# A two-layer hybrid trunk on one core: x loaded first, work ahead of the first matmuls reordered, softplus moved to GpSimd

## The chip, the cores and the metric

The kernel runs on one NeuronCore of a Trainium2 chip. The metric is the device time of one execution in microseconds; lower is better. Engines are called as the profile calls them: PE (TensorE matmul), PEld (its weight loads), DVE (VectorE), ACT (ScalarE), POOL (GpSimd) and SP (SyncE, which here only issues DMAs).

## What is computed

Two layers, 256 positions, width 1024. The part that matters here is the way into a layer and the first things that are made of its projection:

```python
c_act = silu(c)
# per layer
mod = c_act @ ada_w + ada_b;  shift, scale, gate = split(mod, 3)
h = rmsnorm(x, norm_g) * (1 + scale) + shift
z = h @ w_in                       # 13312 columns; all branches read z
q = rope(rmsnorm(b_q, qn_g), pos) * 0.125;  k = rope(rmsnorm(b_k, kn_g), pos)
log_a = -8 * sigmoid(...) * softplus(-lru_lambda)    # RG-LRU branch
...
x = x + gate * (merged @ w_o)
```

Behind z stand three branches: a convolution with a gated recurrence (A), attention over dilated windows (B) and gated linear attention (C). They are multiplied with further weights and merged.

## The kernel before

x is kept transposed: 8 tiles of 128 features by 256 positions. All weights are read once. `stream` cuts them into units in the order of use, which SP loads into six `raw` buffers (512 KB each at most). For each unit ACT makes a rounded copy `whi` (L223) and DVE the rest `wlo` (L224); h is split in the same way into `hhi` and `hlo`, and each product is three matmuls (whi by hhi, wlo by hhi, whi by hlo). `advance` does this split up to three units ahead.

The first 16 units are the columns for q, k, v and the gate of branch B of head pair 0, four pieces of the contraction each (`mm_t`, L789 to 791; `xps` tiles for the gate, L777 to 779). Each piece needs two of the eight tiles of h. The next units are of kind F (`mm_f`, L797 to 799): one unit gives one tile of 128 columns for branch A (`ax`, `ag`).

**adaLN.** The rows of c_act @ ada_w are not made on PE: for each of 16 columns `ada_tile` runs one DVE instruction over a 128 by 1024 weight tile (L325, shown as a custom instruction and a read of its accumulator), then a small product (L327). Columns come in pairs (shift, scale); a pair completes one tile of h: `h_tile` does `tmp` on DVE (L357), `hhi` on ACT (L359), `hlo` on DVE (L360). START spreads the 16 columns over the first 13 units; ten of them land in early buffers named after later tiles (`ada_yhi`, `ada_ylo`, `ada_hraw` and so on).

**rms.** `stats_start` squares x on ACT (L372), adds on DVE (L375, L376) and sums over partitions on PE (L379). `rstd_full` makes the inverse root: `rs_y` on ACT by logarithm and exponential, then a correction with `rs_m` and `rs_q` on DVE (L342, L346 to 348).

**Small constants.** `angles` (L412 to 427) reduces position times frequency and takes sine and cosine; `rope_tables` (L436 to 443) makes eight products of 128 by 192. `softplus` (L390 to 404) is 19 DVE instructions on 128 by 16 with one exponential on ACT. Its results `sp4` and `sp4n` are first used by branch A.

**Evacuation of q and k** (`evac_qk`, L552 to 560). For each half of the positions DVE multiplies the PSUM bank with two tables into `ra` and `rb` (two buffers each) and reduces the squares to `ss`; POOL adds `ra` and `rb` into `ro` (L557, L558), scales `ss` (L559) and takes its power (L560); DVE multiplies `ro` with it (L565). There are four such halves for pair 0 (q twice, then k twice). F units write the PSUM banks that these halves free (pool `pmm`, 4 banks).

**Order.** A scheduler that simulates time puts the instructions of each engine in a row; an engine runs its row in order and waits at its head. `tc.issue_after` only forces an order between two instructions. SP issues loads in the order written, as buffers come free.

## Time and profile before

| | us |
|---|---|
| median of 3 runs | 910.96 (910.28 to 912.53) |
| the profiled execution | 912.47 |
| its span, first to last instruction | 910.7 |
| PE busy in the span | 872.9 (96%) |
| DVE busy | 673.0 (74%) |
| ACT busy | 532.0 (58%) |
| POOL busy | 175.1 (19%) |
| mean granted TensorE clock | 0.996 of full speed |

The span is cut into 40 slices of some 23 us, and the digits below are tenths of busy time in each. PE is full everywhere but in the first slice; DVE is nearly full in the first four.

```profile
## 2 busy tenths in 40 slices
PE   3989999999999999999999999989999999999998
PEld 3978999999988888999889999989999988899998
DVE  6998898669666667666775888986896666656674
```

### The profile page before, as it was taken

The numbers are of one execution on the slowest core, as the hardware profiler recorded it, in microseconds if no ns is written. First come the engines' busy times: TensorE is split into PE (matmuls) and PEld (weight loads), VectorE is DVE, ScalarE is ACT, GpSimd is POOL, SyncE is SP. The second block draws the span as 40 slices with busy tenths as digits, with TensorE's granted clock in tenths as the row PEclk, the third lists the DMA queues.
The fourth block names the chain that finished last, engine by engine and source line by source line (L and its number), as shares of the span: only waits on it lengthen the run. The fifth ranks groups of instructions, "written<-read, shape, count | busy, mean of one in ns | idle before, by whom it ended". The sixth has DMA issues, their size and how long they took to land.

```text
span 910.7 us, 16407 instructions
## 1 busy us (share of the span) xinstructions
PE 872.9 (96%) x6340; PEld 825.3 (91%) x6340; DVE 673.0 (74%) x1115; ACT 532.0 (58%) x897; POOL 175.1 (19%) x160
## 2 busy tenths in 40 slices
PE   3989999999999999999999999989999999999998
PEld 3978999999988888999889999989999988899998
DVE  6998898669666667666775888986896666656674
...
GB/s 328 317 279 139 145 165 207 132 136 201 240 189 191 202 212 205 208 238 206 224 152 160 177 145 145 179 195 109 190 206 232 160 190 163 150 173 185 188 163 47
DMA packets 52111, 170.16 MB, mean 187 GB/s; under 512 B 6240, under 2 KB 8160, under 8 KB 52032
## 3 DMA queue, kind: packets, MB, share of 16 engines
...
q0 software_dynamic: 144, 0.20, 0.2%
...
## 4 chain that ended last, share of the span: by engine, by line
PE 57%; DVE 18%; DMA 10%; issue 7%; ACT 5%; POOL 3%; SPq 0%; DVEq 0%; ACTq 0%
PE mm L797 10%; PE mm L799 10%; PE mm L798 10%; DMA raw<-in_ada_dram 8%; DVE wlo L224 7%; PE mm L791 6%; PE mm L790 6%; PE mm L789 6%; PE xps L172 1%; ACT whi L223 1%; POOL ss L560 1%; PE xps L168 1%; DVE raw L325 1%; DVE rb L554 1%; DVE ra L552 1%
## 5 line engine op out<-in xcount | busy, mean ns | idle before, releaser
L224 DVE TENSOR_TENSOR wlo<-raw,whi 128x1024 fp32r<-128x1024 f32 (+2 forms) x288 | 335.6, 1173 | 86.9 <-ACT whi L223 85.5
L223 ACT CAST whi<-raw 128x1024 fp32r<-128x1024 f32 (+2 forms) x288 | 280.2, 977 | 189.5 <-PE mm L798 123.6
L797 PE MATMUL mm<-hhi,whi 128*128 128x256 f32 x768 | 217.8, 284 | 3.3 <-DVE rb L554 3.2
L799 PE MATMUL mm<-hhi,wlo 128*128 128x256 f32 x768 | 216.6, 282 | 3.1 <-DVE wlo L224 3.1
L798 PE MATMUL mm<-hlo,whi 128*128 128x256 f32 x768 | 216.0, 281 | 0.0
L789 PE MATMUL mm<-whi,hhi 128*128 128x384 f32 (+2 forms) x480 | 170.9, 361 | 7.2 <-ACT hhi L359 6.5
L790 PE MATMUL mm<-wlo,hhi 128*128 128x384 f32 (+2 forms) x480 | 173.0, 362 | 1.4 <-DVE wlo L224 1.2
L791 PE MATMUL mm<-whi,hlo 128*128 128x384 f32 (+2 forms) x480 | 169.1, 358 | 0.5 <-DVE hlo L360 0.5
L797 PEld LDWEIGHTS mm<-hhi,whi 128*128 128x128 f32 x768 | 144.6, 188 | 5.3 <-ACT tmp L847 3.6
L799 PEld LDWEIGHTS mm<-hhi,wlo 128*128 128x128 f32 x768 | 144.5, 188 | 4.3 <-DVE wlo L224 3.7
L798 PEld LDWEIGHTS mm<-hlo,whi 128*128 128x128 f32 x768 | 144.8, 189 | 0.4
L789 PEld LDWEIGHTS mm<-whi,hhi 128*128 128x128 f32 x480 | 93.4, 195 | 15.3 <-ACT hhi L359 7.9
L790 PEld LDWEIGHTS mm<-wlo,hhi 128*128 128x128 f32 x480 | 93.9, 196 | 9.1 <-DVE wlo L224 2.8
L325 DVE CUSTOM_DVE_ANT_0 raw<-raw,crow,vec_sb 128x1024 f32<-128x1024 f32 x38 | 48.7, 1283 | 70.7 <-DMA raw<-in_ada_dram 70.7
L791 PEld LDWEIGHTS mm<-whi,hlo 128*128 128x128 f32 x480 | 92.7, 194 | 7.2 <-DVE hlo L360 0.8
L797 PE MATMUL mm<-yhi,whi 128*128 128x256 f32 x320 | 89.9, 281 | 2.1 <-DVE mg L939 2.1
L798 PE MATMUL mm<-ylo,whi 128*128 128x256 f32 x320 | 89.3, 279 | 0.0
L799 PE MATMUL mm<-yhi,wlo 128*128 128x256 f32 x320 | 89.2, 279 | 0.0
L797 PEld LDWEIGHTS mm<-yhi,whi 128*128 128x128 f32 x320 | 60.4, 189 | 3.1 <-DVE mg L939 2.3
L799 PEld LDWEIGHTS mm<-yhi,wlo 128*128 128x128 f32 x320 | 60.2, 188 | 0.8 <-DVE mrg L905 0.8
L798 PEld LDWEIGHTS mm<-ylo,whi 128*128 128x128 f32 x320 | 60.1, 188 | 0.0
L698 POOL TENSOR_TENSOR at_hl<-att_sb,at_hl 128x384 fp32r<-128x384 f32 x8 | 8.8, 1096 | 207.1 <-ACT at_hl L697 207.1
...
## 6 DMA issues: line engine op xcount, KB each, us to landing
raw<-in_ws_dram SPq DMA_DIRECT2D x192, 512.0 KB, 4.0
...
```

The source lines that it names most:

```text
L168: seen[0] = T.matmul(*a, **k).ins
L172: seen[0] = T.transpose(*a, **k).ins
L223: A.copy(hi, r)
L224: V.tensor_tensor(lo, r, hi.bitcast(F32), ALU.subtract)
L325: V.tensor_tensor_reduce(w, w, crow2, 1.0, b, ALU.mult, ALU.add, a if i == 0 else m)
L552: V.tensor_tensor(ra.rearrange("p (g s) d -> p g s d", g=3), z4, ctab[l][:, i, t].unsqueeze(2).to_broadcast(bc), ALU.mult)
L789: T.matmul(o, ah, wh, start=(k == 0), stop=False)
L790: T.matmul(o, ah, wl, start=False, stop=False)
L791: T.matmul(o, al, wh, start=False, stop=(k == KT - 1))
L797: T.matmul(ps[:, 0:S], hi[:, a:b], xh[:, k], start=(k == 0), stop=False)
L798: T.matmul(ps[:, 0:S], hi[:, a:b], xl[:, k], start=False, stop=False)
L799: T.matmul(ps[:, 0:S], lo[:, a:b], xh[:, k], start=False, stop=(k == nk - 1))
```

## The change

Six things are changed, all in the first tenth of the program (layer 1 keeps its code).

- The three small loads `eye`, `pos` and `inv` go out on the ACT queue, ahead of ACT's table load; on SP x follows c at once. `pos` and `inv` had been loaded by SP behind the fourth adaLN column.
- `angles` keeps the reduction and runs between `diag` and the sums of squares; `sines` has the sine, the cosine and what follows. The eight table products of 192 columns become four of 384.
- Adding 1 to the scale biases (`b1`) moves behind the sums of squares.
- For layer 0 columns 2 to 15 of adaLN, and the `wlo` of units 0 to 3, are ordered behind the first `tmp` of h; the `whi` of units 1 to 3 behind the first `hhi`.
- `softplus` runs on GpSimd but for one reciprocal on DVE and three ACT functions, and is started at unit 4 in place of 16. Multiply-and-add pairs become two instructions, as GpSimd gets single operations. The scaling of `vec_sb` at V_ON goes to GpSimd too.
- `warm_up` gives PE two matmuls on `diag` and three on `rs_m`, whose results nobody reads.

```diff
@@ advance
-                    if it[1] < 4:
-                        st.enter_context(tc.issue_after(cur["ra"]))
-                        st.enter_context(tc.issue_after(cur["rv"]))
+                    if it[1] < 4:
+                        st.enter_context(tc.issue_after(cur["h0a" if it[1] else "ra"]))
                     A.copy(hi, r)
+                with ExitStack() as st:
+                    if it[1] < 4:
+                        st.enter_context(tc.issue_after(cur["h0v"]))
                     V.tensor_tensor(lo, r, hi.bitcast(F32), ALU.subtract)
@@ loads
-    SY.dma_start(out=eye_sb, in_=eye)
+    for t, s in ((eye_sb, eye), (pos_sb, pos), (inv_sb, inv.partition_broadcast(P))):
+        A.dma_start(out=t, in_=s)
@@ ada_tile
+        with ExitStack() as st:
+            if l == 0 and 2 <= c < 16:
+                st.enter_context(tc.issue_after(cur["h0v"]))
+            V.tensor_tensor_reduce(w, w, crow2, 1.0, b, ALU.mult, ALU.add, a if i == 0 else m)
@@ stats_start
-                V.tensor_tensor(sq[i - 1], sq[i - 1], t, ALU.add)
-        V.tensor_tensor(sq[0], sq[0], sq[2], ALU.add)
+                with tc.issue_after(cur["an"]):
+                    V.tensor_tensor(sq[i - 1], sq[i - 1], t, ALU.add)
+        v = V.tensor_tensor(sq[0], sq[0], sq[2], ALU.add)
+        b1 = vec_sb[:, :, V_ADA:V_ADA + 16].rearrange("p l (j i) -> p l j i", i=2)[:, :, :, 0]
+        with tc.issue_after(v.ins):
+            V.tensor_scalar(b1, b1, 1.0, None, ALU.add)
@@ softplus
-        V.scalar_tensor_tensor(e, lam, -1.0, lam, ALU.mult, ALU.max)
+        A.activation(e, lam, AF.Abs)
         A.activation(e, e, AF.Exp, scale=-1.0)
-        V.tensor_scalar(s, e, 2.0, None, ALU.add)
+        G.tensor_scalar(s, e, 2.0, None, ALU.add)
         V.reciprocal(s, s)
-        V.tensor_scalar(p, s2, 1.0 / 17.0, None, ALU.mult)
-        for k in range(7, 0, -1):
-            V.scalar_tensor_tensor(p, p, 1.0 / (2 * k + 1), s2, ALU.add, ALU.mult)
+        G.tensor_scalar(p, s2, 1.0 / 17.0, 1.0 / 15.0, ALU.mult, ALU.add)
+        for k in range(6, -1, -1):
+            G.tensor_tensor(p, p, s2, ALU.mult)
+            G.tensor_scalar(p, p, 1.0 / (2 * k + 1), None, ALU.add)
...
@@ rope_tables
-            for t in range(2):
-                V.tensor_tensor(ct[:, i, t].rearrange("p g (e d) -> p g e d", e=2), g,
-                                cs[:, t].unsqueeze(1).unsqueeze(1).to_broadcast([P, 3, 2, 32]), ALU.mult)
+            V.tensor_tensor(ct[:, i].rearrange("p t g (e d) -> p t (g e) d", e=2),
+                            g.unsqueeze(1).to_broadcast([P, 2, 6, 32]),
+                            cs.unsqueeze(2).to_broadcast([P, 2, 6, 32]), ALU.mult)
...
@@ start of the program
+    with tc.issue_after(cur["diag"]):
+        angles()
+    warm_up(diag[:, 0:2].rearrange("p k n -> p (k n)"), 2)
     sts = stats_start()
-    rstd = rstd_full(sts)
+    rstd = rstd_full(sts, 3)
...
-    sts = layer(0, h, {2: tables, 15: load_small, 16: small})
+    sts = layer(0, h, {2: tables, 4: small, 15: load_small})
```

**DVE at the start**, between the sum over partitions and the first tile of h. `ada_yhi` and `ada_ylo` are adaLN columns 0 to 3 and ISA is the adaLN instruction; before:

```order
L342 TENSOR_SCALAR rs_m<-xps 128x256
L325 ISA ada_ylo,acc<-ada_ylo,crow,vec_sb 128x1024
L325 ISA acc 128x1
L346 TENSOR_TENSOR rs_q<-rs_y 128x256
L325 ISA ada_ylo,mod<-ada_ylo,crow,vec_sb 128x1024
L325 ISA mod 128x1
L327 TENSOR_TENSOR mod<-acc,vec_sb 128x1
L347 TENSOR_TENSOR rs_q<-rs_q,rs_m 128x256
L348 SCALAR_TENSOR_TENSOR rs_y<-rs_q,rs_y 128x256
L224 TENSOR_TENSOR wlo<-raw,whi 128x800
L357 SCALAR_TENSOR_TENSOR tmp<-x_sb,mod,rs_y 128x256 x2
```

The same place on DVE after the change:

```order
L346 TENSOR_SCALAR rs_m<-xps 128x256
L350 TENSOR_TENSOR rs_q<-rs_y 128x256
L351 TENSOR_TENSOR rs_q<-rs_q,rs_m 128x256
L352 SCALAR_TENSOR_TENSOR rs_y<-rs_q,rs_y 128x256
L361 SCALAR_TENSOR_TENSOR tmp<-x_sb,mod,rs_y 128x256
L329 ISA ada_ylo,acc<-ada_ylo,crow,vec_sb 128x1024
L329 ISA acc 128x1
L329 ISA ada_ylo,mod<-ada_ylo,crow,vec_sb 128x1024
L329 ISA mod 128x1
L226 TENSOR_TENSOR wlo<-raw,whi 128x800
```

The correction of the root and the first `tmp` now stand ahead of two adaLN columns and of the first `wlo`.

**POOL ahead of the first evacuation.** The rows from POOL's first work (`a_sb`, a small weight of branch C) to the first power of `ss`; before:

```order
L469 TENSOR_TENSOR a_sb<-a_raw,a_sb 16x512
L557 TENSOR_TENSOR ro<-ra,rb 128x6x32
L558 TENSOR_TENSOR ro<-ra,rb 128x6x32
L456 TENSOR_TENSOR t_622<-t_597,t3r 128x2x16
L557 TENSOR_TENSOR ro<-ra,rb 128x6x32
L558 TENSOR_TENSOR ro<-ra,rb 128x6x32
L559 TENSOR_SCALAR ss<-ss 128x12
L560 TENSOR_TENSOR ss<-ss,mhalf 128x12
```

After, the end of the softplus chain (`spl`, `sp`, `sp4n`) on POOL and the same evacuation behind it:

```order
L408 TENSOR_TENSOR spl_401<-spl_401,spl_400 128x16
L409 TENSOR_SCALAR spl_401<-spl_401 128x16
L484 TENSOR_TENSOR a_sb<-a_raw,a_sb 16x512
L410 TENSOR_TENSOR spl_401<-spl_401,spl_399 128x16
L412 TENSOR_SCALAR spl_401<-spl_401 128x16
L413 TENSOR_TENSOR spl_401<-spl_401,spl_398 128x16
L414 TENSOR_SCALAR sp_149<-spl_401 128x16
L415 TENSOR_SCALAR sp4n<-spl_401 128x16
L572 TENSOR_TENSOR ro<-ra,rb 128x6x32
L573 TENSOR_TENSOR ro<-ra,rb 128x6x32
L471 TENSOR_TENSOR t_658<-t_633,t3r 128x2x16
```

Ahead of the first shown row stand 18 more small POOL instructions (`hb`, the V_ON scaling, the head of the chain); the first additions into `ro` are now behind all of them.

**DVE from the first half of q to the third.** Before:

```order
L552 TENSOR_TENSOR ra<-mm,ctab 128x384
L554 TENSOR_TENSOR rb<-mm,stab 128x384
L556 TENSOR_REDUCE ss<-sqq 128x6
L398 SCALAR_TENSOR_TENSOR spl_785<-spl_785,spl_784 128x16
L224 TENSOR_TENSOR wlo<-raw,whi 128x1024
L398 SCALAR_TENSOR_TENSOR spl_785<-spl_785,spl_784 128x16
L224 TENSOR_TENSOR wlo<-raw,whi 128x1024
L398 SCALAR_TENSOR_TENSOR spl_785<-spl_785,spl_784 128x16
L224 TENSOR_TENSOR wlo<-raw,whi 128x1024
L848 SCALAR_TENSOR_TENSOR sgb<-tmp,xps 128x256
```

The same stretch after the change, to the third `ra`:

```order
L567 TENSOR_TENSOR ra<-mm,ctab 128x384
L569 TENSOR_TENSOR rb<-mm,stab 128x384
L571 TENSOR_REDUCE ss<-sqq 128x6
L226 TENSOR_TENSOR wlo<-raw,whi 128x1024 x3
L567 TENSOR_TENSOR ra<-mm,ctab 128x384
L569 TENSOR_TENSOR rb<-mm,stab 128x384
L571 TENSOR_REDUCE ss<-sqq 128x6
L863 SCALAR_TENSOR_TENSOR sgb<-tmp,xps 128x256
L226 TENSOR_TENSOR wlo<-raw,whi 128x1024 x2
L892 SCALAR_TENSOR_TENSOR ya<-mm,vec_sb,ya 128x255
L567 TENSOR_TENSOR ra<-mm,ctab 128x384
```

The `spl` rows between are gone from DVE; the rest keeps its order, but one `wlo` and one `sgb` that stood ahead of the second half's `ra` now stand behind it.

## Rows read from the trace of the kernel before

Columns of the first view: stretch in us, its length, then PE, PEld, DVE, ACT and POOL, the granted clock, the DMA share and GB/s. Columns of a timeline: start, us busy, engine, line, operation, output from inputs, and in brackets the idle time before and its releaser.

**Rows 1.** Busy us of each engine (xinstructions) by stretch of the span.
```profile
12.00:20.00 8.00, 1.94 (x4) 1.03 (x4) 7.71 (x17) 3.56 (x6) 0.00 (x0) 1.00 1.03 407
20.00:40.00 20.00, 19.59 (x115) 19.58 (x116) 20.00 (x39) 8.21 (x12) 0.00 (x0) 1.00 0.88 328
60.00:82.00 22.00, 17.32 (x135) 16.09 (x133) 21.61 (x47) 15.35 (x32) 15.13 (x14) 1.00 0.49 155
82.00:100.00 18.00, 17.28 (x134) 16.53 (x134) 14.08 (x25) 15.26 (x27) 4.95 (x4) 1.00 0.45 138
```

**Rows 2.** Waits, 0 to 100 us: us in total, times, longest.
```profile
PE mm L797 <- DVE rb L554: 3.2, 2, 2.6
```

**Rows 3.** Timeline of DVE, 4 to 22 us.
```profile
9.19 0.69 DVE L375 TENSOR_TENSOR sq<-sq 128x512 f32<-128x512 f32 x1 [4.64 <-ACT sq L372]
...
11.66 1.28 DVE L325 CUSTOM_DVE_ANT_0 ada_yhi<-ada_yhi,crow,vec_sb 128x1024 f32<-128x1024 f32 x1
...
19.33 0.88 DVE L357 SCALAR_TENSOR_TENSOR tmp<-x_sb,mod,rs_y 128x256 f32<-128x256 f32 x2
```

**Rows 4.** Timeline of PE, 8 to 26 us.
```profile
20.41 0.70 PE L789 MATMUL mm<-whi,hhi 128*128 128x400 f32 x1 [6.47 <-ACT hhi L359]
...
21.91 0.84 PE L789 MATMUL mm<-whi,hhi 128*128 128x384 f32 x2
...
25.59 0.52 PE L791 MATMUL mm<-whi,hlo 128*128 128x384 f32 x2
```

**Rows 5.** Loads of x, issued by SP: duration min, median, max in ns.
```profile
L240 SPq DMA_DIRECT2D x_sb<-in_x_t_dram x2: 424/430/435, 1.6 to 2.1; - x2
```

**Rows 6.** Timeline of DVE, 36 to 61 us.
```profile
45.32 0.22 DVE L421 SCALAR_TENSOR_TENSOR an<-an,an 128x64 f32<-128x64 f32 x1
45.45 0.48 DVE L360 SCALAR_TENSOR_TENSOR hlo<-tmp,mod,hhi 128x256 fp32r<-128x256 f32 x1
...
54.82 0.62 DVE L440 TENSOR_TENSOR ctab<-gq,cs 128x192 f32<-128x192 f32 x2
...
56.97 1.22 DVE L224 TENSOR_TENSOR wlo<-raw,whi 128x1024 fp32r<-128x1024 f32 x1
58.10 1.51 DVE L360 SCALAR_TENSOR_TENSOR hlo<-tmp,mod,hhi 128x256 fp32r<-128x256 f32 x1
59.54 0.16 DVE L390 SCALAR_TENSOR_TENSOR spl<-vec_sb 128x16 f32<-128x16 f32 x1
```

**Rows 7.** Timeline of DVE, 61 to 100 us.
```profile
61.20 0.55 DVE L552 TENSOR_TENSOR ra<-mm,ctab 128x384 f32<-128x384 f32 x1
...
74.61 1.28 DVE L565 TENSOR_TENSOR ro<-ro,ss 128x768 f32<-128x768 f32 x1
...
76.78 0.54 DVE L554 TENSOR_TENSOR rb<-mm,stab 128x384 f32<-128x384 f32 x1
...
79.66 1.21 DVE L224 TENSOR_TENSOR wlo<-raw,whi 128x1024 fp32r<-128x1024 f32 x1
```

**Rows 8.** Timeline of POOL, 0 to 100 us.
```profile
56.54 2.79 POOL L469 TENSOR_TENSOR a_sb<-a_raw,a_sb 16x512 fp32r<-16x512 f32 x1 [54.55 <-ACT a_sb L468]
62.36 0.60 POOL L557 TENSOR_TENSOR ro<-ra,rb 128x192 f32<-128x192 f32 x1 [3.02 <-DVE rb L554]
...
71.91 0.20 POOL L559 TENSOR_SCALAR ss<-ss 128x12 f32<-128x12 f32 x1
72.19 2.31 POOL L560 TENSOR_TENSOR ss<-ss,mhalf 128x12 f32<-128x12 f32 x1
...
79.72 1.22 POOL L559 TENSOR_SCALAR ss<-ss 128x12 f32<-128x12 f32 x1
```

**Rows 9.** Timeline of PE, 76 to 78 us: the start of the fourth F unit.
```profile
76.58 0.50 PE L475 MATMUL xps<-t1t,a_sb 48*128 48x256 f32 x2
...
77.31 0.36 PE L797 MATMUL mm<-hhi,whi 128*128 128x256 f32 x1
```

**Rows 10.** Loads into raw buffers, 11 to 60 us, from issue.
```profile
DMA to landing us min/median/max: 4.0/5.7/9.4
```

42 lines of the change are left out of this document (21 added, 21 removed).

## The prediction

> **What bounds the kernel now.** I read the page's slices first: PE is at 9 tenths everywhere but in the first slice, so a gain can only come from the start, or from what the start hands on. Next the busy time by stretch [rows 1]. The reader should see two engines there. PE has 1.94 us of work in 12 to 20, is full in 20 to 40 (19.59 of 20), loses 4.7 of 22 us in 60 to 82, and from 82 on is nearly full again. DVE has 7.71 of 8, then 20.00 of 20, then 21.61 of 22, and only after 82 does it get air (14.08 of 18). So from its first adaLN instruction at 11.66 [rows 3] to about 82 us DVE never rests, and PE, busy as it looks, is fed by it. The timelines say how. PE's first layer matmul starts at 20.41 after 6.47 us of waiting for `hhi` [rows 4], which waits for DVE's first `tmp` at 19.33 [rows 3]. Later PE waits 3.2 us, 2.6 in one piece, for `rb`, the evacuation that frees a PSUM bank for an F unit [rows 2]. The fourth F unit starts at 77.31, just as the fourth `rb` (76.78 plus 0.54) is done [rows 7, 9]. That is the last place where DVE as a whole holds PE; the 0.73 us of PE work from 76.58 to 77.31 [rows 9] stands ahead of this unit in both orders, but after the change it fits into the wait. What counts is therefore when the fourth `rb` ends, against 76.58.
>
> **The start.** x no longer waits behind `eye`: one SP issue of 0.43 us [rows 5]. The angle instructions fall into DVE's 4.64 us of idle time ahead of the squares [rows 3] and are covered; they are about 1.1 us long, and without this cover they would delay the first adaLN by as much. First adaLN: about 11.35 for 11.66. The first `tmp` then has only two adaLN instructions and the four short root steps ahead of it, instead of four and a `wlo`; summing the same rows along the new order ends it at 16.0 and puts PE's first layer matmul at about 16.6, **3.8 us earlier**. That is PE's lead, not yet a gain: the same DVE work still has to be done before PE can finish the first 16 units. The five added matmuls lie in PE's wait of 6.47 and cost nothing. Of ACT's three added DMA issues, about 0.4 each like SP's [rows 5], only c and `crow` could come late; they are ready before the squares.
>
> **DVE up to the first evacuation.** What leaves this stretch, against the first `ra` at 61.20 [rows 7]: 0.3 by the earlier start; nine angle instructions that move into idle time, at 0.13 start to start (45.32 to 45.45 [rows 6], others 0.07 to 0.15), 1.1; of the nine softplus instructions in 59.54 to 61.20 [rows 6, 7], 1.66 together, one stays, so 1.5; the tables, eight of 192 columns in 2.15 (54.82 to 56.97 [rows 6]), become four of 384, 0.3 less by the 0.55 of a 384-column `ra` [rows 7]; and `hlo` at 58.10 took 1.51 [rows 6], because POOL's `a_sb` ran from 56.54 for 2.79 [rows 8], where an undisturbed one takes 0.48 [rows 6], so 1.0. Sum 4.2: first `ra` at **57.0**, called E. A bound on the other side: in the new order DVE reaches the thirteenth adaLN column at 48.6, whose buffer a `wlo` frees at 45.6; the quickest load takes 4.0 [rows 10], so up to 1.2 of waiting, and E lies between 57.0 and 58.2.
>
> **DVE from E to the fourth `rb`.** Before, 61.20 to 77.3 is 16.1. Eight more softplus instructions leave it, some 1.5, so 14.6. If nothing else came in between, the fourth `rb` would end at 71.6 to 72.8, 3.7 to 4.9 before 76.58.
>
> **POOL comes in between.** Softplus is now 24 POOL instructions on 128x16, 22 of them behind the one reciprocal that stays on DVE, with `a_sb` among them: 23 rows from about E-6.3. The additions into `ro` stand behind all of these, and the third `ra` needs the buffer that the first pair of additions gives back. What is one such row worth? The trace has two prices for the same instruction, L559 on 128x12. With DVE not on a two-input instruction it took 0.20, and 0.28 to the next start [rows 8]. Beside a `wlo` (79.66, 1.21 long [rows 7]) it took 1.22 [rows 8] and ended when the `wlo` did. `a_sb` and `hlo` held each other in the same manner. So I read: a DVE instruction with two SBUF inputs and a POOL instruction take turns, one of mine, one of yours. In the 6.3 us before E DVE runs nine or ten of these (adaLN, `wlo`, `hlo`, `tmp`), so nine or ten POOL rows get through. The evacuation reads PSUM and leaves POOL free (1.4 us, five rows at 0.28), the next three `wlo` let three through, the second evacuation takes `a_sb`, and the last five rows end at about E+9.7. Two additions of 0.60 [rows 8] follow: the third `ra` starts at E+10.9, and not at E+9.2. Then POOL has the second half's additions, the small `t`, `ss` and its power of 2.31 [rows 8]; DVE's `ro` (1.28 [rows 7]) waits for it until E+15.1, and one `wlo`, `ra` and `rb` later the fourth `rb` ends at E+18.2, that is **75.2 to 76.4**. Of 3.7 to 4.9 us of gain 0.2 to 1.4 are left. A later wait, for the gates of branch A, hangs on the same POOL rows, and moves by half a us at most. I take 0.7.
>
> The Trainium skill, GPSIMD Engine Reference, section 8 (Key points), says that GpSimd shares its SBUF interfaces with VectorE, with contention where DVE has two SBUF inputs; by this rule the sum is the one above, and it speaks against putting softplus there beside `wlo`. The trace agrees in the 1.22 against 0.20.
>
> **Rivals.** A: *POOL is not held.* Rows of 16 columns may slip in where one of 12 did not, since DVE has a gap between instructions. At 0.28 the 23 rows end at about E+1, as the first additions become due, and the fourth `rb` is at 71.6 to 72.8: 3.7 to 4.9 faster, 906.1 to 907.3. For it: two instances at 0.2 to 0.3. Against it: the 1.22, and both long `ro` additions beside `wlo`. The same skill page, section 4.1 (Engine selection), puts GpSimd at about twice DVE's time for two inputs; by that, from 0.18 a row, 23 rows are an estimate of 8.5 us, done at E+2.2, and the result would also be A's.
>
> B: *PE's whole lead arrives.* 3.8 us from the start, and up to 1.9 from the cold matmuls: at 20.41 to 24 PE runs with two 384-column matmuls in 0.84 instead of 0.52 [rows 4], 0.16 each for 12, the 1.2 GHz level after 6.47 us of idling. Together 5.7: 905.3. Against it: DVE rests nowhere between 11.66 and 82 [rows 1], so a PE that is early or quick only waits longer; it would need the evacuations to be no bound. The Trainium skill, TensorE: Matmul & The Clock Gate, Part 1, says that an idle array drops to half clock and that work issued ahead brings it back; here that could be right and still pay nothing.
>
> C, the slower side: *POOL holds DVE.* Each turn costs DVE too: `hlo` was 1.0 longer beside `a_sb`, and if each of some 18 small POOL rows keeps DVE off for 0.06 to 0.15, that is 1 to 2.7 us more before E and behind it, with the load's 1.2 on top. The fourth `rb` then comes at 77.4 to 80: 1 to 3.5 slower, 912 to 914.5. It decides where this `rb` ends later than 77.3.
>
> D: *it doesn't do what it says.* If the reciprocal waits on DVE for POOL and ACT, everything queued behind it (the `wlo` of units 12 to 15) stands; this ends like C.
>
> **How the numbers follow.** The profiled execution took 912.47, with 1.8 around its span, and lies 1.5 above the median of 910.96; the change in the stretch is taken off the median. Main case, POOL takes DVE's place as the bound: 910.96 - 0.7 = **910.3**, itself 909 to 912; chance 0.50. A 0.28, B 0.05, C and D 0.17. About 0.3%, 2.7 us, is what a measurement of this kernel can tell from no change. Faster (under 908.2) is A and B: 0.33. Slower (over 913.7) is the upper part of C and D: 0.10. Same: 0.57. The range leaves out B and the worst of C: from A's 906.0 to 913.2.
>
> **What would show it.** In the changed kernel's profile: first adaLN near 11.35, first layer matmul near 16.6 and at full clock sooner; no angle or `spl` rows on DVE after 57 but the reciprocal; first `ra` at 57 to 58.2; small POOL rows of about 1.2 beside `wlo` and 0.2 beside `ra`; idle time on DVE ahead of the third `ra` and of `ro`, released by POOL; the fourth F unit at 75.2 to 76.4. `spl` rows of 0.2 throughout mean A; `wlo` and adaLN that are longer than 1.22 and 1.28 mean C. I'm wrong in kind if the fourth F unit moves and the end does not move with it, or the other way round.

## The result: 0.67% slower, and the profile after

The changed kernel takes 917.36 us in the median of six runs (915.68 to 922.33) against 911.08 (910.28 to 912.86) for the kernel before on the same chips: a ratio of **1.0067, 95% interval 1.0041 to 1.0092**, by this ratio some 6.1 us slower. 910.3 was forecast, with a range that ended at 913.2. The profiled execution took 918.53 with a span of 916.4 (before: 912.47 and 910.7). The granted clock does not explain it: over all timed runs it averages 0.993 after and 0.990 to 0.993 before.

First the busy time by stretch of the changed kernel (columns as in [rows 1]):

```profile
12.00:20.00 8.00, 4.55 (x13) 3.57 (x14) 7.72 (x17) 3.41 (x6) 0.00 (x0) 0.67 1.03 408
20.00:40.00 20.00, 16.10 (x87) 14.12 (x86) 20.00 (x36) 7.75 (x12) 0.00 (x0) 0.96 0.84 315
60.00:82.00 22.00, 17.82 (x135) 16.95 (x134) 19.20 (x30) 13.00 (x28) 18.52 (x27) 1.00 0.59 197
82.00:100.00 18.00, 18.00 (x144) 17.43 (x144) 12.75 (x21) 15.33 (x26) 3.01 (x3) 1.00 0.42 129
```

Against [rows 1]: PE has 2.6 us more in the first stretch, three of the five warm-up matmuls (six rows) among it, and 3.5 us less in the second. So its lead is spent between 20 and 40. In 60 to 82 DVE rests 2.8 us, POOL is busy for 18.5.

**The start.** DVE's timeline from 5 to 20 us, for [rows 3]:

```profile
5.89 0.17 DVE L425 CAST an<-pos_sb 128x2 f32<-128x2 int32 x1 [0.35 <-DMA pos_sb<-in_pos_dram]
9.48 0.41 DVE L427 TENSOR_SCALAR an<-inv_sb,an 128x32 f32<-128x32 f32 x2 [3.42 <-DMA inv_sb<-in_inv_dram]
...
13.59 1.28 DVE L329 CUSTOM_DVE_ANT_0 ada_yhi<-ada_yhi,crow,vec_sb 128x1024 f32<-128x1024 f32 x1
...
17.78 0.48 DVE L361 SCALAR_TENSOR_TENSOR tmp<-x_sb,mod,rs_y 128x256 f32<-128x256 f32 x1
```

The first adaLN instruction is at 13.59, not 11.35 (before: 11.66): the angles stand in front of DVE's queue and wait 3.42 us for `inv`. The view of the DMA issues from 0 to 12 us says why (size, then median us from issue to landing):

```profile
x_sb<-in_x_t_dram SPq DMA_DIRECT2D x2, 512.0 KB, 6.0
...
eye_sb<-in_eye_dram ACTq DMA_DIRECT2D x1, 64.0 KB, 2.1
...
pos_sb<-in_pos_dram ACTq DMA_DIRECT2D x1, 1.0 KB, 4.7
inv_sb<-in_inv_dram ACTq DMA_DIRECT2D x1, 16.0 KB, 7.7
```

`inv` is 16 KB, third on ACT's queue, and lands 7.7 us after its issue, beside the first loads of x. PE's timeline from 16 us, and its idle times from 20 to 62 (for [rows 4]):

```profile
16.55 2.93 PE L154 MATMUL mm<-rs_m,ones 128*128 128x256 f32 x6 [1.94 <-DVE rs_m L346]
18.91 1.87 PE L804 MATMUL mm<-whi,hhi 128*128 128x400 f32 x4
...
26.18 0.39 PE L794 MATMUL xps<-hhi,wlo 128*128 128x256 f32 x1 [1.36 <-DVE wlo L226]
30.66 1.00 PE L806 MATMUL mm<-whi,hlo 128*128 128x400 f32 x4 [0.90 <-DVE hlo L366]
34.18 0.99 PE L804 MATMUL mm<-whi,hhi 128*128 128x400 f32 x4 [0.99 <-ACT hhi L364]
...
47.61 0.39 PE L792 MATMUL xps<-hhi,whi 128*128 128x256 f32 x1 [1.42 <-ACT whi L222]
```

The first layer matmul comes at 18.91, 1.5 us ahead of before, and PE then waits for `wlo`, `hlo`, `hhi` and `whi`, 5.5 us in six pieces up to 62 us (four are shown), where before it waited twice (0.7 for `whi`, 0.5 for `hlo`).

**The first evacuation.** DVE from 58 to 79 us, for [rows 6, 7]:

```profile
58.19 1.23 DVE L226 TENSOR_TENSOR wlo<-raw,whi 128x1024 fp32r<-128x1024 f32 x1
62.76 0.56 DVE L567 TENSOR_TENSOR ra<-mm,ctab 128x384 f32<-128x384 f32 x1 [3.33 <-ACT sqq L562]
...
72.78 0.54 DVE L567 TENSOR_TENSOR ra<-mm,ctab 128x384 f32<-128x384 f32 x1
...
75.22 1.08 DVE L580 TENSOR_TENSOR ro<-ro,ss 128x768 f32<-128x768 f32 x1
...
78.24 0.54 DVE L569 TENSOR_TENSOR rb<-mm,stab 128x384 f32<-128x384 f32 x1
```

DVE is done at 59.4 and waits 3.33 us for ACT's squares of q (`sqq`), and those wait for PE: its last q matmuls run from 61.8 to 62.7. The first `ra` starts at 62.76 for 61.20 before. From there to the end of the fourth `rb` at 78.78 DVE never stands idle, and needs 16.0 us, as before (16.1).

POOL beside it, for [rows 8]:

```profile
58.43 1.10 POOL L409 TENSOR_SCALAR spl<-spl 128x16 f32<-128x16 f32 x1
59.62 0.22 POOL L408 TENSOR_TENSOR spl<-spl,spl 128x16 f32<-128x16 f32 x1
...
64.22 1.23 POOL L413 TENSOR_TENSOR spl<-spl,spl 128x16 f32<-128x16 f32 x1
...
66.70 1.17 POOL L415 TENSOR_SCALAR sp4n<-spl 128x16 f32<-128x16 f32 x1
67.94 0.59 POOL L572 TENSOR_TENSOR ro<-ra,rb 128x192 f32<-128x192 f32 x1
...
69.03 0.26 POOL L471 TENSOR_TENSOR t<-t,t3r 128x32 f32<-128x32 f32 x1
```

Beside a `wlo` a row of 16 columns takes 1.10 to 1.23, in DVE's gap 0.22. The chain ends at 67.87; only then come the first additions into `ro`, and behind them `t` of branch A's gates, 4.5 us later than before (64.54). PE does not wait for it: `t` is ready at 69.3, and its transposes stand behind the third F unit and start at 76.87 (before: 72.58).

**The gates of branch A.** Their two pairs of PE matmuls, and on DVE their last sum (`la`) and the root scan of branch A (`rt`):

```profile
81.36 0.50 PE L490 MATMUL xps<-t1t,a_sb 48*128 48x256 f32 x2
87.05 0.50 PE L490 MATMUL xps<-t1t,a_sb 48*128 48x256 f32 x2
...
94.79 1.22 DVE L499 TENSOR_TENSOR la<-la,laxs 128x1024 f32<-128x1024 f32 x1 [2.68 <-ACT la L497]
...
132.37 1.85 DVE L540 TENSOR_TENSOR_SCAN rt<-rt,ya 128x256 f32<-128x256 f32 x3
```

Before these were at 76.58 [rows 9], 81.95, 91.46 and 128.10. PE's order has changed too: the transposes of `t` and the pairs stand one F unit further back. PE also has three idle times from 120 to 152 us, 2.0 us together, where before there are none of this size:

```profile
132.60 0.85 PE L172 MATMUL xps<-eye_sb,ro 128*128 128x128 f32 x6 [0.32 <-DVE ro L580]
135.12 0.45 PE L805 MATMUL mm<-wlo,hhi 128*128 128x384 f32 x1 [0.62 <-DVE wlo L226]
148.93 0.45 PE L805 MATMUL mm<-wlo,hhi 128*128 128x384 f32 x1 [1.04 <-DVE wlo L226]
```

That DVE comes to these `wlo` late because the late scan pushes in among them is not shown: f1 (below) has the scan at 129.53 and still 1.6 us of such waits, at 133 to 139, and e11, which is level with the kernel before, has 1.7. Measured by the start of the same `wlo`, the changed kernel lies between 1.8 us ahead and 2.3 behind from 85 to 127 us, mostly 2.2 to 2.8 behind from 131 to 142, and 3.4 to 3.6 behind from 144 to 163. Some 1.6 more goes at 168 to 172, where this execution has two windows at about half clock. From 174 to the end the lag stays between 3.2 and 5.7.

### The profile page after: what moved, and what is told of

Same layout as the page of the kernel before. It is cut to its first block, busy times and chain, and to the rows that moved or that the text cites. A ratio compares the mean times of both kernels' runs of the same rounds, so it can differ in the third digit from the quotient of the medians.

```text
span 916.4 us, 16435 instructions
## 1 busy us (share of the span) xinstructions
PE 876.1 (96%) x6350; PEld 828.6 (90%) x6350; DVE 671.0 (73%) x1088; ACT 531.8 (58%) x899; POOL 190.4 (21%) x185
## 4 chain that ended last, share of the span: by engine, by line
PE 55%; DVE 18%; DMA 11%; issue 7%; ACT 4%; POOL 3%; DVEq 0%; ACTq 0%
PE mm L812 10%; DMA raw<-in_ada_dram 10%; PE mm L814 10%; PE mm L813 10%; DVE wlo L226 8%; PE mm L805 5%; PE mm L806 5%; PE mm L804 5%; PE xps L172 2%; POOL ss L575 1%; ACT whi L222 1%; PE xps L168 1%; DVE rb L569 1%; PE ps_s L168 1%; DVE ra L567 1%
## 5 line engine op out<-in xcount | busy, mean ns | idle before, releaser
L814 PE MATMUL mm<-hhi,wlo 128*128 128x256 f32 x768 | 218.9, 285 | 0.8 <-DVE wlo L226 0.7
L813 PE MATMUL mm<-hlo,whi 128*128 128x256 f32 x768 | 218.5, 285 | 0.0
L805 PE MATMUL mm<-wlo,hhi 128*128 128x384 f32 (+2 forms) x480 | 170.3, 356 | 3.5 <-DVE wlo L226 3.2
L806 PE MATMUL mm<-whi,hlo 128*128 128x384 f32 (+2 forms) x480 | 167.1, 355 | 0.9 <-DVE hlo L366 0.9
L812 PEld LDWEIGHTS mm<-hhi,whi 128*128 128x128 f32 x768 | 147.8, 192 | 6.1 <-ACT whi L222 2.2
L814 PEld LDWEIGHTS mm<-hhi,wlo 128*128 128x128 f32 x768 | 147.7, 193 | 1.8 <-DVE wlo L226 1.2
L813 PEld LDWEIGHTS mm<-hlo,whi 128*128 128x128 f32 x768 | 147.9, 193 | 0.4
L329 DVE CUSTOM_DVE_ANT_0 raw<-raw,crow,vec_sb 128x1024 f32<-128x1024 f32 x38 | 48.6, 1280 | 69.4 <-DMA raw<-in_ada_dram 69.4
```

The source lines that it names most:

```text
L329: V.tensor_tensor_reduce(w, w, crow2, 1.0, b, ALU.mult, ALU.add, a if i == 0 else m)
L805: T.matmul(o, ah, wl, start=False, stop=False)
L806: T.matmul(o, al, wh, start=False, stop=(k == KT - 1))
L812: T.matmul(ps[:, 0:S], hi[:, a:b], xh[:, k], start=(k == 0), stop=False)
L813: T.matmul(ps[:, 0:S], hi[:, a:b], xl[:, k], start=False, stop=False)
L814: T.matmul(ps[:, 0:S], lo[:, a:b], xh[:, k], start=False, stop=(k == nk - 1))
```

## The experiments

All were timed in three rounds against the kernel before on the same chip. Times are us; `ra` is DVE's first evacuation, `t` the subtraction ahead of branch A's gates, `la` their last sum, scan the root scan. E is the start of the first `ra`. "Late start" means that `inv` comes as in the changed kernel.

| kernel | ratio (95%) | median, before | `ra` | `t` | `la` | scan |
|---|---|---|---|---|---|---|
| before | 1 | | 61.20 | 64.54 | 91.46 | 128.10 |
| after | 1.0067 (1.0041 to 1.0092) | 917.36, 911.08 | 62.76 | 69.03 | 94.79 | 132.37 |
| e4 | 0.9997 (0.9980 to 1.0014) | 911.59, 911.47 | 61.52 | 64.78 | 91.79 | 128.40 |
| e2 | 1.0092 (1.0062 to 1.0121) | 920.17, 911.47 | 62.96 | 66.29 | 95.58 | 133.13 |
| e5 | 1.0068 (1.0043 to 1.0092) | 918.62, 912.54 | 63.03 | 69.31 | 95.06 | 132.62 |
| e3 | 1.0075 (1.0047 to 1.0103) | 919.16, 911.47 | 62.89 | 66.97 | 95.25 | 133.11 |
| f1 | 1.0060 (1.0036 to 1.0084) | 917.76, 912.54 | 62.73 | 69.02 | 92.23 | 129.53 |
| g1 | 1.0076 (1.0047 to 1.0104) | 919.16, 911.56 | 62.84 | 66.91 | 91.75 | 129.05 |
| g2 | 1.0064 (1.0042 to 1.0086) | 917.47, 911.56 | 62.67 | 66.02 | 92.92 | 129.30 |
| e10 | 1.0044 (1.0025 to 1.0063) | 915.12, 911.47 | 58.72 | 67.94 | 94.25 | 129.32 |
| e9 | 1.0067 (1.0044 to 1.0090) | 918.93, 911.56 | 64.16 | 68.74 | 96.46 | 134.04 |
| h2 | 1.0052 (1.0035 to 1.0069) | 915.46, 910.54 | 63.82 | 67.16 | 96.36 | 131.72 |
| h3 | 1.0063 (1.0045 to 1.0080) | 916.53, 910.54 | 63.14 | 66.48 | 95.62 | 133.27 |
| e6 | 1.0036 (1.0023 to 1.0049) | 913.85, 910.54 | 61.01 | 62.24 | 92.00 | 130.18 |
| f2 | 1.0020 (1.0008 to 1.0033) | 914.71, 912.54 | 58.86 | 67.95 | 91.75 | 129.31 |
| e11 | 1.0001 (0.9985 to 1.0017) | 912.84, 912.54 | 59.29 | 60.52 | 90.30 | 128.37 |
| f3 | 0.9997 (0.9977 to 1.0016) | 911.83, 911.56 | 59.44 | 60.68 | 86.36 | 122.42 |
| i1 | 1.0066 (1.0045 to 1.0086) | 917.12, 912.08 | 63.87 | 70.31 | 96.78 | 131.78 |
| i2 | 1.0004 (0.9986 to 1.0022) | 913.20, 912.08 | 60.30 | 61.53 | 91.30 | 129.54 |
| i3 | 1.0000 (0.9987 to 1.0013) | 912.00, 912.08 | 59.85 | 61.09 | 86.76 | 122.70 |

### Softplus alone (e4, e2)

e4 is the kernel before with the softplus of the change, started at unit 4; e2 is the changed kernel with the softplus of before, at unit 16 (the V_ON scaling goes with it in both):

```diff
-            A.activation(e, lam, AF.Abs)
+            V.scalar_tensor_tensor(e, lam, -1.0, lam, ALU.mult, ALU.max)
...
-        for k in range(6, -1, -1):
-            G.tensor_tensor(p, p, s2, ALU.mult)
-            G.tensor_scalar(p, p, 1.0 / (2 * k + 1), None, ALU.add)
+        for k in range(7, 0, -1):
+            V.scalar_tensor_tensor(p, p, 1.0 / (2 * k + 1), s2, ALU.add, ALU.mult)
...
-    sts = layer(0, h, {2: tables, 4: small, 15: load_small})
+    sts = layer(0, h, {2: tables, 15: load_small, 16: small})
```

> The kernel before with softplus alone moved to POOL and started at unit 4. Theory P: slower by 3 to 5, 914 to 916, with `t` at 67 to 69 and la about 3 us late. Theory S: no slower than before, 910 to 911.5, since DVE loses 3 us of work.

> The changed kernel with softplus put back on DVE at unit 16, all else as changed. Theory P (POOL's row is the cause: the small subtraction `t` and `a_sb` stand behind the softplus chain, so the la chain is 3.5 us late): `t` back to about 64 to 66 us, first `la` sum on DVE back to about 91 instead of 94.8, no PE waits for `wlo` at 134 and 147; 911 to 913. Theory S (the start is the cause: DVE waits 3.4 us for `inv` with the sums of squares behind it): as slow as the change, 916 to 918. Theory C (small POOL rows hold DVE): DVE rows before the first evacuation no longer, about 1 us back, 915.

Softplus on GpSimd costs nothing in the kernel before, and taking it back gains nothing in the changed one (1.0092 and 1.0067 can't be told apart). In e2 the first `ra` is still at 62.96: what came late there was never POOL. DVE also waits as long at the start, 3.55 us, though the operand that it is said to wait for is now `vec_sb`, for the V_ON scaling.

### The warm-up (e5)

```diff
-    warm_up(diag[:, 0:2].rearrange("p k n -> p (k n)"), 2)
     sts = stats_start()
-    rstd = rstd_full(sts, 3)
+    rstd = rstd_full(sts)
```

> The changed kernel without the five extra matmuls, in the same order on every engine. If they cost something on PE's path (they stand ahead of the first layer matmul at half clock): 0.5 to 1 better, 916. If they do bring the clock up earlier: the first layer matmuls stay at half clock longer and it is up to 1 slower. If DVE feeds PE anyway: the same, 917.

1.0068 against 1.0067: the five matmuls neither cost nor give. With them the granted clock from 16 to 22 us is 0.50 to 0.60, the lower level, and the first layer matmuls run at it (four of 400 columns in 1.87). Without them these are as slow (1.74), and PE stays slow for longer. The same two matmuls, in the changed kernel and in e5:

```profile
21.76 0.53 PE L805 MATMUL mm<-wlo,hhi 128*128 128x400 f32 x2
```

```profile
22.15 0.87 PE L805 MATMUL mm<-wlo,hhi 128*128 128x400 f32 x2
```

In e5 the full pace comes only at 25.2 us. (The column of the granted clock reads 1.00 for e5 there, so the level is read from the durations.) The Trainium skill, TensorE: Matmul & The Clock Gate, Part 1, has activity release the throttle; the trace agrees in that PE was at full pace 3.4 us sooner with the five matmuls. It paid nothing: PE then waits 1.36 us for `wlo`, against 0.41 in e5, and goes on at 26.2 and 26.5.

### Branch A's gates with the late start (e3, f1, g1, g2)

e3 takes the two subtractions ahead of the gates from GpSimd to DVE; f1 leaves them and puts the gates' PE work ahead of the third, fourth and fifth F unit; g1 is both, g2 is e2 with f1.

```diff
-        G.tensor_tensor(t3[:, :, 16:32], t1, t3r.bitcast(F32), ALU.subtract)
+        (G if l else V).tensor_tensor(t3[:, :, 16:32], t1, t3r.bitcast(F32), ALU.subtract)
```

```diff
-            T.matmul(ps[:, 0:S], hi[:, a:b], xh[:, k], start=(k == 0), stop=False)
+            with ExitStack() as st:
+                if k == at:
+                    st.enter_context(tc.issue_after(cur["la", n]))
+                T.matmul(ps[:, 0:S], hi[:, a:b], xh[:, k], start=(k == 0), stop=False)
...
+                fu = {("ax", 1): (0, 0), ("ag", 1): (0, 1), ("ax", 2): (0, 2)}.get((nm, p), (None, 0)) if l == 0 else (None, 0)
```

> The changed kernel with only two POOL instructions of layer 0, the subtractions into `a_sb` and `t`, given to DVE; softplus stays on POOL. Theory P: `t` at about 65 to 66, la chain 3 us earlier, 912 to 914, though the additions into `ro` stay behind softplus. Theory S: 916 to 918. If it is the additions into `ro` that matter (the forecast's third half waiting), also 916 to 918.

> The changed kernel with the la chain's PE work of layer 0 forced ahead again: the two transposes of `t` before the third F unit, the first pair of la products before the fourth, the second before the fifth. Theory Q (in the changed row they stand one unit later, la is 3.3 us later whatever POOL does, and branch A's DVE work then stands ahead of `wlo` at 132 to 148): la's sum on DVE at 91 to 92 instead of 94.8, no PE waits for `wlo` at 134 and 147, lag against before at 151 us 1.5 instead of 3.5; 914 to 915.5. Theory S (the start alone) and theory W (the clock of PE alone): 916 to 918.

> The changed kernel with both: the subtractions into `a_sb` and `t` on DVE (off POOL's row behind softplus), and the la chain's PE work forced ahead of the third, fourth and fifth F units. Theory Q+P (la is late by its place in PE's row, and `t` by its place in POOL's, and either alone keeps it late): `t` at 67, la sum at 91, no wait of PE for `t`, no waits for `wlo` at 134 to 148, lag against before at 151 us about 1.5 to 2; 913.5 to 915 on a before of 911. Theory that the loss is only the start and the clock: as the change, +6.

> The changed kernel with softplus on DVE and la's PE work forced ahead; the late start (inv) stays. Against softplus on DVE alone (+0.92%): theory Q: la sum at 91 to 92 instead of 95.6, lag at 151 us about 2 instead of 4.3, +0.4%. Theory that la's place does not matter: stays at +0.9%.

All four are misses. f1, g1 and g2 bring `la` and the scan back by 1.9 to 3.3 us, and the time stays at 1.0060 to 1.0076: with the first `ra` at 62.7 PE stands still earlier instead, in f1 for 2.7 us ahead of the transposes of `t` at 74.67 (the trace names no releaser). In g1 it names one for the same place:

```profile
75.18 0.40 PE L474 MATMUL xps<-eye_sb,t 128*48 128x128 f32 x2 [2.37 <-DVE sgb L866]
```

So PE waits there for DVE's `sgb`, which reads an `xps` bank and stands behind the third `ra`, and not for `t`, which is ready at 67.5. In all five kernels with this order (f2 and f3 are below) the transposes start 0.5 us after this `sgb` does, in f1 at 74.67 after 74.16, whatever releaser is named. e3 fits: with `t` 2.1 us earlier than in the changed kernel, `la` is no earlier.

### The start (e10, e9, h2, h3, e6)

e10 is the changed kernel with `inv` and `pos` as 34 further columns of `eye`: one load for three.

```diff
-    eye_sb = one.tile([P, P], F32, name="eye_sb")
-    pos_sb = one.tile([P, 2], I32, name="pos_sb")
-    inv_sb = one.tile([P, 32], F32, name="inv_sb")
+    eyx = one.tile([P, P + 34], F32, name="eye_sb")
+    eye_sb, inv_sb, pos_sb = eyx[:, 0:P], eyx[:, P:P + 32], eyx[:, P + 32:P + 34].bitcast(I32)
...
-    for t, s in ((eye_sb, eye), (pos_sb, pos), (inv_sb, inv.partition_broadcast(P))):
-        A.dma_start(out=t, in_=s)
+    A.dma_start(out=eyx, in_=eye)
```

e9 instead puts the angles behind the root:

```diff
-                with tc.issue_after(cur["an"]):
-                    V.tensor_tensor(sq[i - 1], sq[i - 1], t, ALU.add)
+                V.tensor_tensor(sq[i - 1], sq[i - 1], t, ALU.add)
...
-    with tc.issue_after(cur["diag"]):
-        angles()
...
     rstd = rstd_full(sts, 3)
+    with tc.issue_after(cur["rv"]):
+        angles()
```

> The changed kernel with inv and pos carried in the load of eye (one DMA of 128x162 on the ACT queue, replicated rows in the host layout). Theory S: no wait for inv, first adaLN at 11.4 instead of 13.6, first evacuation 2 us earlier; 913.5 to 915.5 if the rest of the loss is POOL's row, 911 if the start is all of it. Theory P: the softplus chain starts 2 us earlier too, so part of the gain comes through `t`; if the start does not matter at all, 916 to 918.

> The changed kernel, loads as changed, with the angle instructions behind the root instead of ahead of the sums of squares, so that nothing on DVE waits for inv. Theory S: first adaLN at 11.4 instead of 13.6, the 1.1 us of angle work back on DVE's path; +0.4 to +0.5%, as with the single load. If the order around la decides alone (its PE rows stand late here as in the change): +0.6%, no better.

In e10 the first adaLN comes at 11.07 and the first `ra` at 58.72, near the places forecast (11.35, 57.0 to 58.2), and 0.23 of the 0.67% are gone, though the two intervals overlap. Now DVE does wait for POOL, which it never does here in the changed kernel; its third `ra` and the first `ro`:

```profile
68.02 0.56 DVE L565 TENSOR_TENSOR ra<-mm,ctab 128x384 f32<-128x384 f32 x1 [1.37 <-POOL ro L571]
72.86 1.35 DVE L578 TENSOR_TENSOR ro<-ro,ss 128x768 f32<-128x768 f32 x1 [1.54 <-POOL ss L573]
```

e10's POOL row of `t`, its PE rows, and its stretches (as [rows 1]):

```profile
67.94 0.25 POOL L469 TENSOR_TENSOR t<-t,t3r 128x32 f32<-128x32 f32 x1
```

```profile
72.13 0.38 PE L472 MATMUL xps<-eye_sb,t 128*48 128x128 f32 x2
74.05 0.50 PE L488 MATMUL xps<-t1t,a_sb 48*128 48x256 f32 x2 [1.53 <-ACT t1t L474]
76.73 0.58 PE L810 MATMUL mm<-hhi,whi 128*128 128x256 f32 x1 [2.18 <-DVE rb L567]
```

```profile
72.00:74.00 2.00, 0.51 (x5) 0.23 (x3) 1.14 (x1) 1.80 (x4) 2.00 (x3) 1.00 0.49 183
74.00:76.00 2.00, 0.50 (x2) 0.29 (x2) 2.00 (x4) 0.84 (x2) 0.66 (x1) 0.78 0.00 0
76.00:78.00 2.00, 1.27 (x6) 1.27 (x7) 2.00 (x6) 0.00 (x0) 1.16 (x3) 0.50 0.58 172
78.00:80.00 2.00, 2.00 (x11) 2.00 (x11) 2.00 (x4) 0.00 (x0) 1.92 (x2) 0.50 0.07 25
80.00:82.00 2.00, 2.00 (x12) 2.00 (x12) 1.00 (x3) 0.40 (x1) 2.00 (x2) 0.51 0.65 197
```

PE starts the third F unit at 69.19, 4.4 us ahead of before (73.57). It takes up `t` right behind it, without a wait, then stands still twice, for ACT's `t1t` and for `rb`, which comes late behind DVE's two waits for POOL. It starts the fourth F unit at 76.73, 0.6 us ahead of before (77.31), and runs at about half clock to 82; the fifth starts at 82.57, 2.3 us behind (80.23).

e9 was a miss: its first adaLN is at 12.02, but PE's waits before 62 us are 7.9 (5.5 after), and its first `ra` comes at 64.16. h2 and h3 test the start in the kernel before: the small loads on ACT, x first, the angles ahead of the sums of squares, nothing else; h3 with the single load.

```diff
-    SY.dma_start(out=eye_sb, in_=eye)
+    for t, s in ((eye_sb, eye), (pos_sb, pos), (inv_sb, inv.partition_broadcast(P))):
+        A.dma_start(out=t, in_=s)
...
+                with tc.issue_after(cur["an"]):
+                    V.tensor_tensor(sq[i - 1], sq[i - 1], t, ALU.add)
...
+    with tc.issue_after(cur["diag"]):
+        angles()
     sts = stats_start()
...
-            load_after(("sy", "a", 3), (pos_sb, pos), (inv_sb, inv.partition_broadcast(P)))
-            angles()
+            sines()
```

e6 is e2 with `inv` on SP ahead of x:

```diff
-    for t, s in ((eye_sb, eye), (pos_sb, pos), (inv_sb, inv.partition_broadcast(P))):
+    SY.dma_start(out=inv_sb, in_=inv.partition_broadcast(P))
+    for t, s in ((eye_sb, eye), (pos_sb, pos)):
```

> The kernel before with the change's start alone: eye, pos and inv on the ACT queue, x first on SP, angle instructions ahead of the sums of squares; adaLN order, softplus, tables and no extra matmuls as before. Here la's PE work stands early. If the wait for inv is by itself the largest piece of the loss: first adaLN near 13.6, slower than before by 2 to 4 us. If it only costs together with the change's other parts: 911 to 912.

> The same with inv and pos in eye's load: first adaLN near 11.3. If the wait for inv is the lever: 909 to 911.5, 2 to 4 better than with three loads. La's PE work stands late in this schedule; if la's place is the larger lever, it is the slower of the two.

> The changed kernel with softplus on DVE, and inv loaded by SP ahead of x (eye and pos on the ACT queue, tensors as before). If the single load helped by when inv lands, and not by the shape of its tensor: as with the single load and softplus on DVE, within 0.3% of before; else +0.9%, as with softplus on DVE alone.

h2 shows that the change of the start costs 0.52% by itself, in a kernel with softplus on DVE. h3 shows that `inv` is not the whole of it: loaded early, the start still costs 0.63%, though its first adaLN is at 11.53, no later than before. (In both, the 1 is still added to the scale biases among the angles, and DVE waits for `vec_sb` there, 3.21 and 2.86 us.) DVE's order comes out differently in h3 from 20 us on, its `wlo` of units 4 and 5 from 31.99 for 29.15, and the first `ra` is at 63.14 again. e6 lies between (0.36%), but it does not test `inv` alone. There `inv` lands 3.3 us after its issue, in time, and DVE waits among the angles all the same, for the operand of the V_ON scaling:

```profile
9.01 0.17 DVE L984 TENSOR_SCALAR vec_sb<-vec_sb 128x4 f32<-128x4 f32 x1 [3.23 <-DMA vec_sb<-in_vec_dram]
```

Its first adaLN is at 12.44, between e10's and the changed kernel's.

### The single load with the rest undone (f2, e11, f3)

f2 is e10 with f1's order, e11 is e10 with e2's softplus, f3 is all three; the edits are those above.

> The same row of PE together with inv and pos in eye's load. Theory Q plus S: 911.5 to 913.5, no wait at the start and la early. Theory W (PE, early and starved, idles for about 4 us near 72 to 77 and then runs at half clock to 82): no better than the single load alone, 914.5 to 916.

> The changed kernel with the single load and softplus on DVE. Theory that POOL's row still matters once the start is mended (fourth `rb` waits for `ro`, released by POOL): better than the single load alone, 912 to 914. Theory that DVE's own work is the bound there: the same or worse, 915 to 918. Theory W: it follows whether PE idles long enough between 65 and 80 us to lose its clock.

> The changed kernel with the single load, softplus on DVE, and la's PE work forced ahead. There la is early already without force (sum at 90.3), so theory Q expects little beyond the single load with softplus on DVE: within 0.2% of before. If the forced row takes away the PE waits near 137 and 143: up to 2 us faster than before.

With the first `ra` early, softplus on DVE, which did nothing before, gives 0.43% (e11 against e10, the intervals apart), and e11 is level with the kernel before. The gates' order gives 0.24% (f2 against e10), but these two intervals overlap. e11's DVE has neither of e10's two waits for POOL, and its fourth `rb` ends at E+15.3 for E+18.0. Its row for `t`, against 67.94 in e10:

```profile
60.52 0.25 POOL L467 TENSOR_TENSOR t<-t,t3r 128x32 f32<-128x32 f32 x1 [2.75 <-ACT t3r L464]
```

f3 has the gates 4 us earlier than e11 and gains no more.

### The second tile of h (i1, i2, i3)

One more suspect for PE's lost lead: the second `tmp`, 19.73 before, stands at 26.04 in the changed kernel, behind four `wlo` and an adaLN column, so that the first units hold their buffers longer; SP waits 8.3 us in one piece for a `wlo` (longest such wait before: 1.6, from 20 to 50 us). i1 is the changed kernel with that order restored, i2 and i3 the same on e11 and f3:

```diff
                     if it[1] < 4:
-                        st.enter_context(tc.issue_after(cur["h0v"]))
+                        st.enter_context(tc.issue_after(cur["h1v"]))
...
             if l == 0 and 2 <= c < 16:
-                st.enter_context(tc.issue_after(cur["h0v"]))
+                st.enter_context(tc.issue_after(cur["h0v" if c < 4 else "h1v"]))
...
         cur.setdefault("h0v", v.ins)
+        cur[f"h{j}v"] = v.ins if l == 0 else cur.get(f"h{j}v")
```

> The changed kernel with one order restored: the second tile of h (tmp, line 361) stands right behind the first and ahead of wlo of units 0 to 3 and of adaLN columns 4 to 15, as in the kernel before; loads, angles, softplus on GpSimd and the rest stay as changed. Theory S (the second tile, at 26.04 in the changed kernel against 19.73 before, keeps units 0 to 3 in their buffers until 31, so whi of unit 4 waits 4.3 us for PE, SP waits 8.3 us for a wlo, the DMA share in 28 to 36 us is 0.64 against 0.84, and PE loses 2.9 us of work in 20 to 36): second tmp near 22, SP's longest wait under 6, PE busy over 14 of the 16 us, first ra at 60 to 61.5 for 62.76, and a ratio of 1.002 to 1.005. Rival R (the late adaLN columns and the late la row keep the end where it is): the start of the stretch improves, the first ra and the end do not, ratio 1.006 to 1.007.

> The changed kernel with inv and pos in eye's load, softplus back on DVE at unit 16, and the second tile of h right behind the first; against the kernel with the first two alone (ratio 1.0001) only the last differs. Theory S: first ra at 56 to 58.5 for 59.29, the DMA share in 28 to 36 over 0.78 for 0.72, ratio 0.996 to 0.998. Rival R: PE or DVE behind the first evacuation sets the time, ratio 0.999 to 1.001.

> The same with the la branch's PE work ahead of the third to fifth F unit as well; against the kernel without the last edit (ratio 0.9997, la sum at 86.36, root scan at 122.42) only the second tile's place differs. Theory S: ratio 0.995 to 0.998. Rival R: 0.999 to 1.001.

Refuted. i1's second `tmp` starts at 21.25, but the third then comes at 34.97 and the first evacuation later still:

```profile
63.87 0.55 DVE L568 TENSOR_TENSOR ra<-mm,ctab 128x384 f32<-128x384 f32 x1
```

Nothing changes in the ratio of any of the three. The same DVE work in another order moves the wait to another tile.

### What the runs say together

Two conditions sort the kernels. Those whose first `ra` comes after 62.6 (after, e2, e3, e5, e9, f1, g1, g2, h2, h3, i1) are all at 1.0052 to 1.0092, whatever else is undone. Of those with a first `ra` at 61.6 or earlier, the ones whose `t` comes at 67.9 (e10, f2) lose 0.20 to 0.44%, and those whose `t` comes by 64.8 (e4, e11, f3, i2, i3) lose nothing; e6, with 0.36%, fits only half, and its start lies between. `t` is only a mark here of where POOL's softplus chain ends, since PE does not wait for it. So the loss has two causes in series: the start, which makes the first evacuation late, and softplus on POOL, which DVE waits for once the evacuation is early. Undoing the second alone gains nothing while the first holds. That late gates cost time is not shown. And nothing goes below the kernel before: f3 and i3 have the first `ra` 1.4 to 1.8 us, the fourth F unit 2.5 to 3.0 us and the scan over 5 us earlier, and take the same time.

That both causes act is shown by pairs whose intervals stand apart: the edits of e2 and e11 differ in the load alone (1.0092, 1.0001), so do those of f1 and f2 (1.0060, 1.0020), and those of e10 and e11 in softplus alone (1.0044, 1.0001). That the late first `ra` is itself the price of the start, and not a companion of it, is the reading of the eleven kernels, not proved apart. Open stays where 2 to 3 us of the changed kernel's 6 go behind 160 us: the lag there is 3.5, the mean clock is that of before, and executions of one kernel lie 1.4 to 8.6 us apart. Open too is why the lead of some 3 us that f3 shows at 162 us is not in its median: its profiled execution, 907.66, was its shortest of ten (to 913.37).

## Why the prediction was wrong, step by step

- **The start.** "The angle instructions fall into DVE's 4.64 us of idle time" failed. They fall into it only if `inv` is there. I weighed ACT's three added issues by their 0.4 us and asked whether c and `crow` would be late; I never asked when `inv` lands. [rows 10] had the prices, 4.0, 5.7 and 9.4 us from issue to landing: with `inv` issued at 1.65 and 1.9 us of angles behind it (the forecast had 1.1), the median ends them at 9.2, just with the idle time, and the longest at 12.9. These are prices of larger loads. I gave this no bounds; it took 7.7. First adaLN 13.59 for 11.35, first layer matmul 18.91 for 16.6. With the single load (e10) the first adaLN is at 11.07 and the first `tmp` ends at 15.7, against 16.0 in the sum: the working of this step was right but for the landing.
- **DVE up to the first evacuation.** The sum for E, 57.0 to 58.2, assumed that DVE would still be the last. DVE did the shorter work (45.1 us busy from 14 to 62 for 47.4 before) and was ready at 59.4, but PE was not: E was 62.76. "PE that is early or quick only waits longer" was right about the lead, but it did wait, those 5.5 us, and each piece that does not fall on the slack of the other engine moves its end. With `inv` early E was 58.72 (e10).
- **POOL comes in between.** The price of a row held: 1.10 to 1.23 beside two-input DVE instructions, 0.22 to 0.30 in gaps. In the changed kernel itself POOL is not the bound: the signs named for it, idle time of DVE ahead of the third `ra` and of `ro`, are missing, since softplus ended at E+5.1 there. With E early it ends at E+8.1, and they are there. In e10 the third `ra` starts at E+9.3, `ro` at E+14.1, and the fourth `rb` ends at E+18.0, or 76.7, for E+10.9, E+15.1, E+18.2 and 75.2 to 76.4. The Trainium skill, GPSIMD Engine Reference, section 8 (Key points), tells of this sharing, and the rows agree, 1.10 to 1.23 against 0.22.
- **The gates of branch A, "moves by half a us at most".** As a place this failed too. I hung it on POOL's rows alone. `la` came 3.3 us late in the changed kernel, and not by `t`, for which nobody waits, but by a unit more on PE's queue, which I did not read in the order of instructions. What it costs is not shown: f1 brings `la` back to 92.23, and the time stays.
- **From the fourth F unit to the end.** This is the second step that failed: "the change in the stretch is taken off the median", us for us. The fourth F unit came 1.6 us late (78.92 for 77.31); by that rule the result would have been 912.6, inside the range, and it was 917.4. It fails the other way as well: e10 starts this unit 0.6 us early and is some 4 us slower, and i3 starts it 2.5 us early and takes the same time. In the changed kernel's trace the lag grows to 3.5 us by 144 and to 5.1 by 174. By what is open, but for the 1.6 us at half clock.
- **The warm-up costs nothing**: right (e5).
- **The rivals.** A (POOL not held) is out: the rows between `wlo` take 1.1 to 1.2. B (the lead arrives) is out: it was 1.5 us and is gone by 40 us; and of its 1.9 for cold matmuls, those up to 21.8 us still ran at 0.50 to 0.60 of the clock, and what the rest gained went into PE's next wait. C put the loss in the right place, a fourth `rb` at 77.4 to 80 (it ended at 78.78, and the fourth F unit starts at 78.92 for 77.31), but by the wrong mechanism: no `wlo` beside the last three softplus rows is longer than 1.24 (from 69.4 on, beside `ro` and `ss`, three take 1.53 to 1.62), and what is late at E is PE. D (the reciprocal waits) did not occur. That the later part of the chain could cost more than the first evacuation was in none of them, and so the range ended 4 us short.
